# A two-layer encoder with seven-product matmuls: the products in another order, low halves last, two more chunks a layer by seven products, and fourteen more low parts a layer by DMA

## The chip, the cores and the metric

The kernel runs on one core of a Trainium2 chip. The metric is the device time of one execution in microseconds (us). The kernel before was run three times: 1086.85, 1087.01 and 1087.84 us, median 1087.01 us.

## The reference

The reference is an encoder of two residual layers on one sequence of 512 tokens with 1024 features, all in fp32. Layer 0 mixes tokens with a bidirectional gated linear attention, layer 1 with grouped-query softmax attention. Behind each mixer stands a feed-forward part, which is the place of the change:

```python
def conv_ffn(h, w_up, w_conv, b_conv, w_down):
    u = h @ w_up                      # 1024 -> 2 x 2816
    u = lax.conv_general_dilated(u, w_conv[:, None, :], ..., feature_group_count=u.shape[-1]) + b_conv
    val, gate = jnp.split(u, 2, axis=-1)
    return (jax.nn.silu(gate) * val) @ w_down
...
    x = x + conv_ffn(rmsnorm(x, norm_ffn[i]), ffn_w_up[i], ffn_w_conv[i], ffn_b_conv[i], ffn_w_down[i])
```

The convolution is three taps wide, along the tokens, each feature by itself.

## The kernel before

**Three matmuls for one.** TensorE (PE) multiplies in fp32r. To keep fp32 accuracy every weight piece and every activation is kept as a high part (`hi`, a rounded copy) and a low part (`lo`, what the copy left out), and each product is high by high, high by low and low by high: three matmuls. A weight piece is 128x1024 numbers (512 KB). It is loaded from DRAM into a `raw` tile by a DMA on SP's queue; ScalarE (ACT) copies it into a `wh` tile (`split`, L319), and VectorE (DVE) subtracts the copy from the original into a `wl` tile (L320). The other way is `low_dma` (L271, L272): ACT writes the high part, then ACT writes the negative of the rounded number into `wl`, and a DMA on GpSimd's (POOL's) queue adds the original onto it (`flush`, L308). That takes DVE out of it, and costs ACT a second pass and a DMA. Which pieces go this way is set by tables: `UP_DMA` for chunks by three products, `LOW_0`, `LOW_1`, `LOW_2` for the first, second and third piece of a chunk by seven products.

**The feed-forward part.** The 2816 hidden features are 22 chunks of 128; chunk `m` has a value half and a gate half. A chunk not listed in `SEVEN` is a plain one (`plain_up`): two halves of eight blocks by three matmuls of 512 columns, 48 matmuls. A chunk in `SEVEN` (`seven_up`) computes the same by seven products in place of eight (Strassen's way, in Winograd's form, on 2x2 blocks): each product is four blocks by three matmuls of 256 columns, so 84 matmuls. It needs sums of weight blocks, which `summed` makes on DVE (L293, L294, L283): the first piece holds raw weights (products 1 and 4), the second and third hold sums (products 6 and 2, and 7 and 5), the fourth is half as wide (product 3; ACT L285, DVE L286). It also needs its partial results copied in PSUM: `twice` (L1129) copies product 1 into both halves of a bank `r`, so that products 2 and 6 add onto the two halves `r1` and `r2`; `r2` is copied to `r3` after product 6 (L1095) and after product 5 (L1102); `add_seven` (DVE L1132) adds `r3` to the copied product 7. Then come the convolution (ACT L1117, DVE L1118 and L1119), the silu (ACT L1121), the product of the halves (DVE L1122), and, for chunks 0 to 15, `prepare` (L1145 to L1157, L1138, L1139), which makes the operands of the down-projection.

Parts of the down-projection run inside the chunks: `down_part` (four strips by seven products each, onto x in DRAM through POOL's adding DMAs) begins at chunks 9 and 17 (`DOWN_AFTER`). The rest, `PLAIN`, comes at the end.

**What sets the order.** PE, ACT, DVE, POOL and SP each work through their own list of instructions in order; an instruction whose operand isn't ready holds everything behind it on its engine. The program is written chunk by chunk, with weight pieces made some pieces ahead (`PAW`, `PA`); a scheduler of the framework then sets the order on each engine and the buffers. There are five `raw` tiles, six pairs of `wh` and `wl` from chunk 1 to 19 and four after that, and in PSUM three banks `acc`, two `s` and two `pt`.

In the text, "third piece of chunk 14" means the `wh` and `wl` tiles made from the tile `sum` of that chunk.

Of the kernel before, what the change touches and what calls it, by code (L numbers as in the profile page):

```python
# [66 lines left out]
DOWN_AFTER = {9: 0, 17: 1}  # L67


SEVEN = (6, 7, 8, 10, 11, 12, 13, 15, 16, 18, 19, 20, 21)  # L70
UPA = 3
PA = 4
LOADS = 3
# [1 line left out]
INPUT_AT = {2: (0, 1), 3: (2,), 4: (3,)}  # L75
Q_DMA = ()
UP_DMA = (1, 2, 5)
LOW_0 = (7, 8)
LOW_1 = ()
LOW_2 = ()  # L80
STRIP_0 = ()
STRIP_2 = ()
NR = 5
# [17 lines left out]
def hybrid_encoder_kernel(  # L101
# [39 lines left out]
    def bank(tag, n):  # L141
        return pp.tile([P, S], F32, tag=tag, bufs=PS[tag], name=nm(n))
# [33 lines left out]
    class Weights:  # L176
# [127 lines left out]
        def flush(self):  # L304

            for lo, r in self.pending:
                same = lo.dtype == F32R and r.dtype != F32R
                pool.dma_start(lo.bitcast(F32) if same else lo, r, accum_op=ALU.add)  # L308
            self.pending = []

        def split(self, hi, lo, r, pieces=1, first=False):
# [705 lines left out]
    def ffn(layer, norm, cw, nxt):  # L1017
# [22 lines left out]

        def plain_up(m):

            pss = []
            for t in range(2):
                ps = bank("s" if t else "acc", "up")
                feature_tile(*W.half(up[layer], 2 * m + t, max(UPAW if W.wide else UPA, ahead.get((m, t), 1))), norm.hl if m < SWITCH else fresh, ps)
                pss.append(ps)
                if t == 0 and m not in DOWN_AFTER:
                    begin_up(m + 1)
                if t == 0 and m in DOWN_AFTER:  # L1050
                    down.append(down_part(DOWN_AFTER[m], m))
                    next(down[-1])
# [12 lines left out]
        def product(pieces, src, strip, pairs, i, dst, start):  # L1065
            h, o = PLACE[i]
            if h not in pieces:
                pieces[h] = W.piece(src, strip, h, PAW if W.wide else PA)
            wh, wl = pieces[h]
            for j, p in enumerate(pairs):  # L1070
                sl = slice(o + j * P, o + (j + 1) * P)
                mh, ml = p[i]
                for a, (w, m) in enumerate(((wh, mh), (wh, ml), (wl, mh))):
                    mm(dst, w[:, sl], m, start=start and j == 0 and a == 0, stop=j == len(pairs) - 1 and a == 2,  # L1074
                       skip_group_check=True)
            W.flush()

        def begin_up(m):
            if m in SEVEN:
                begun.append(seven_up(m))  # L1080
                next(begun[-1])

        def seven_up(m):

            pieces = {}
            go = lambda *a: product(pieces, up[layer], m, inputs, *a)
            r = bank("pt", "r1")[:, :H]
            go(1, r, True)
            both = bank("acc", "r")
            r1, r2 = both[:, :H], both[:, H:]  # L1090
            twice(both, r)
            yield
            go(6, r2, False)
            r3 = bank("s", "r3")
            act.activation(r3[:, :H], r2, AF.Copy)  # L1095
# [6 lines left out]
            act.activation(r3[:, H:], r2, AF.Copy)  # L1102
            add_seven(d, r3, r4)
            yield 1, d
            begin_up(m + 1)
            go(2, r1, False)
            go(3, r2, False)
            yield 0, both

# [72 lines left out]
        def down_part(part, m):  # L1182

            pairs = [quads.pop(part * NQ + i) for i in range(NQ)]
            st = {}
            pieces = [{} for _ in range(NQ)]
            go = lambda n, *a: product(pieces[n], w_dn, part * NQ + n, pairs, *a)

            def begin(n):
                r = bank("pt", "r1")[:, :H]
                go(n, 1, r, True)
                st[n] = bank("acc", "r")
                twice(st[n], r)

            begin(0)
            yield
            for n in range(NQ):
                r, c, d = st[n], x_home[n][:, :S], x_home[n][:, S:]  # L1200
                r1, r2 = r[:, :H], r[:, H:]
                go(n, 6, r2, False)
                r3 = bank("s", "r3")
                act.activation(r3[:, :H], r2, AF.Copy)
                r4 = bank("pt", "r4")[:, :H]
                go(n, 7, r4, True)
                g, f = tmp("u", "g"), tmp("u", "f")
                twice(f, r4)
                go(n, 4, r3[:, :H], False)
                go(n, 5, r2, False)  # L1210
                act.activation(r3[:, H:], r2, AF.Copy)  # L1211
                add_seven(f, r3, r4)
                W.pending.append((d, f))
                if n + 1 < NQ:
                    begin(n + 1)
                else:
                    begin_up(m + 1)
                go(n, 2, r1, False)
                go(n, 3, r2, False)
                act.activation(g, r, AF.Copy)  # L1220
                W.pending.append((c, g))

        def end(c, ps):
# [375 lines left out]
```

## Time and profile before

| | |
|---|---|
| three runs, median | 1087.01 us (1086.85 to 1087.84) |
| span of the profiled execution | 1085.5 us; its own time lies among these runs, about 1.5 us above the span |
| PE busy | 1077.5 us |
| DVE busy | 888.5 us |
| ACT busy | 721.1 us |
| POOL busy | 136.7 us |
| DMA | 164.52 MB, 152 GB/s on average |
| feed-forward part of layer 0 | about 223 to 555 us |
| attention of layer 1 | about 555 to 741 us |
| feed-forward part of layer 1 | about 741 us to the end |

The span runs from the first to the last instruction. A busy time counts each instruction from start to end. Instructions of one engine overlap a little: the next one may start before the last has ended, so a stretch of work is costed here by the distance from start to start. A busy PE is not PE at its peak, since the ends of matmuls are modelled.

### The profile page before, as it was taken

How to read it: one execution, taken by the hardware profiler on the slowest of the kernel's cores; microseconds unless marked ns; L12 is line 12 of the kernel's file. 1: busy time of each engine (PE TensorE's matmuls, PEld its weight loads, DVE VectorE, ACT ScalarE, POOL GpSimd, SP SyncE). 2: the span in 40 equal slices, each digit the busy share in tenths (PEclk: the TensorE clock that was granted, in tenths of full speed). 3: DMA queues.
4: the chain of work that ended last, by engine and by line, in shares of the span. 5: the costliest groups of instructions: out<-in, count | busy, mean ns of one | idle time of the engine just before them, and what ended most of it. 6: DMA issues, size and time to landing. Idle time of an engine off the chain costs nothing.

```text
span 1085.5 us, 17391 instructions
## 1 busy us (share of the span) xinstructions
PE 1077.5 (99%) x6672; PEld 966.4 (89%) x6672; DVE 888.5 (82%) x1327; ACT 721.1 (66%) x1134; POOL 136.7 (13%) x153
## 2 busy tenths in 40 slices
PE   9999999999999999999999999999999999999998
PEld 8888988888999999999988888888889999999997
DVE  7998967569898899988755588666989889998882
ACT  8679575478775676666574677656877567666660
POOL 0212112021001100010015333002110010001000
PEclk9999999999999999999999999999999999999999
DMA  8744446499545633274767475549863473227542
GB/s 301 187 126 106 122 141 215 154 207 204 127 125 127 145 120 111 77 177 121 252 149 162 127 204 164 164 158 202 206 148 124 105 166 116 100 80 157 136 175 78
DMA packets 55763, 164.52 MB, mean 152 GB/s; under 512 B 6528, under 2 KB 7040, under 8 KB 55680
## 3 DMA queue, kind: packets, MB, share of 16 engines
q1 hardware_dynamic: 36192, 112.66, 32.2%
q0 software_dynamic: 14592, 42.21, 21.7%
q10 hardware_dynamic: 4896, 8.55, 2.1%
q8 instruction: 52, 0.85, 0.3%
q14 instruction: 31, 0.25, 0.1%
HBM read 114.89 MB, written 14.68 MB: 119 GB/s over the span
## 4 chain that ended last, share of the span: by engine, by line
PE 87%; DVE 6%; ACT 3%; DMA 2%; issue 2%; POOL 0%; SPq 0%; DVEq 0%; ACTq 0%; POOLq 0%
PE r L1074 37%; PE op L535 8%; PE vg L652 7%; PE up L482 4%; PE up L483 4%; PE up L484 4%; PE dn L483 2%; PE dn L484 2%; PE dn L482 2%; PE av L509 1%; PE A L482 1%; DVE wl L320 1%; PE A L484 1%; DMA nl<-xr 1%; PE B L484 1%
## 5 line engine op out<-in xcount | busy, mean ns | idle before, releaser
L320 DVE TENSOR_TENSOR wl<-raw,wh 128x1024 fp32r<-128x1024 f32 x156 | 189.8, 1220 | 31.3 <-ACT wh L319 31.1
L319 ACT ACTIVATE wh<-raw 128x1024 fp32r<-128x1024 f32 x156 | 162.6, 1053 | 73.4 <-PE op L535 20.7
L1074 PE MATMUL r<-gu,wh 128*128 128x256 f32 x896 | 161.2, 282 | 0.0
L1074 PE MATMUL r<-xt,wh 128*128 128x256 f32 x832 | 151.1, 283 | 0.4 <-ACT r L1095 0.3
L1074 PEld LDWEIGHTS r<-gu,wh 128*128 128x128 f32 x896 | 139.3, 190 | 1.0 <-ACT r L1211 0.2
L1074 PEld LDWEIGHTS r<-xt,wh 128*128 128x128 f32 x832 | 129.2, 190 | 1.6 <-ACT r L1095 1.1
L1074 PE MATMUL r<-gu,wl 128*128 128x256 f32 x448 | 126.3, 283 | 0.0
L1074 PE MATMUL r<-xt,wl 128*128 128x256 f32 x416 | 117.2, 283 | 0.0
L1074 PE MATMUL r<-nh,wh 128*128 128x256 f32 x312 | 88.8, 285 | 0.3 <-ACT r L1102 0.3
L1074 PE MATMUL r<-nh,wl 128*128 128x256 f32 x312 | 88.2, 283 | 0.0
L1074 PE MATMUL r<-nl,wh 128*128 128x256 f32 x312 | 87.9, 282 | 0.0
L1074 PEld LDWEIGHTS r<-gu,wl 128*128 128x128 f32 x448 | 85.1, 190 | 0.0
L1074 PEld LDWEIGHTS r<-xt,wl 128*128 128x128 f32 x416 | 79.1, 190 | 0.0
L482 PE MATMUL up<-nh,wh 128*128 128x512 f32 x192 | 75.3, 392 | 0.0
L483 PE MATMUL up<-nl,wh 128*128 128x512 f32 x192 | 75.2, 392 | 0.0
L484 PE MATMUL up<-nh,wl 128*128 128x512 f32 x192 | 75.2, 392 | 0.0
L535 PE MATMUL op<-oT,wh 128*128 128x512 f32 x256 | 72.4, 393 | 0.0
L271 ACT ACTIVATE wh<-raw 128x1024 fp32r<-128x1024 f32 x36 | 38.0, 1056 | 38.2 <-PE up L483 11.5
L1074 PEld LDWEIGHTS r<-nh,wh 128*128 128x128 f32 x312 | 59.3, 190 | 2.9 <-ACT r L1102 2.6
L1074 PEld LDWEIGHTS r<-nl,wh 128*128 128x128 f32 x312 | 59.4, 190 | 0.2
L1074 PEld LDWEIGHTS r<-nh,wl 128*128 128x128 f32 x312 | 59.4, 190 | 0.0
L535 PEld LDWEIGHTS op<-oT,wh 128*128 128x128 f32 x256 | 47.4, 188 | 9.7 <-ACT oT L937 0.3
(299 smaller groups left out, 2761.6 us busy)
## 6 DMA issues: line engine op xcount, KB each, us to landing
raw<-in_w_up_dram SPq DMA_DIRECT2D x84, 512.0 KB, 4.6
raw<-in_w_down_dram SPq DMA_DIRECT2D x44, 512.0 KB, 3.7
wl<-raw POOLq DMA_DIRECT2D x20, 512.0 KB, 5.3
wl<-in_w_up_dram POOLq DMA_DIRECT2D x16, 512.0 KB, 7.8
ring<-p ACTq DMA_DIRECT2D x32, 256.0 KB, 2.6
xw<-in_xw_dram SPq DMA_DIRECT2D x8, 512.0 KB, 6.6
raw<-in_w_v_dram SPq DMA_DIRECT2D x8, 512.0 KB, 5.9
raw<-in_w_g_dram SPq DMA_DIRECT2D x8, 512.0 KB, 4.0
```

The lines of the kernel that those rows point to most:

```text
L271: act.activation(hi, r, AF.Copy)
L319: act.activation(hi[:, sl], a, AF.Copy)
L320: dve.tensor_tensor(lo[:, sl], a, hi[:, sl].bitcast(F32), ALU.subtract)
L482: mm(ps, wh, mh, start=start, stop=False)
L483: mm(ps, wh, ml, start=False, stop=False)
L484: return mm(ps, wl, mh, start=False, stop=stop)
L509: mm(ps[j][:, :width], hl[k][i == 2][:, j * P : (j + 1) * P], (wl if i == 1 else wh)[:, sl], start=k == 0 and i == 0, stop=k == KC - 1 and ...
L535: mm(pss[ng][n], wt[:, sl], mv, start=k == late[0][0] and i == 0, stop=k == late[-1][-1] and i == 2)
L652: last = mm(ps[j], m[:, js], w[:, sl], start=i in (1, 7, 2) and p == 0 and a == 0, stop=i in (4, 2, 3) and p == 3 and a == 2, skip_group_c ...
L1074: mm(dst, w[:, sl], m, start=start and j == 0 and a == 0, stop=j == len(pairs) - 1 and a == 2, skip_group_check=True)
```

## The change

1. Chunks 14 and 17 go by seven products too, in both layers.
2. A product multiplies all its high halves first (eight matmuls) and the low halves last (four); before, the low matmul of each of the four blocks followed its two high ones.
3. The order of a chunk's products, 1, 6, 7, 4, 5, then product 1 of the next chunk, 2, 3, becomes 1, 6, 7, 2, 5, product 1 of the next, 4, 3; the strips of the down-projection change in the same way. The copies of partial results are written into the program ahead of the making of further weight pieces.
4. `LOW_0` grows by ten chunks and `LOW_2` by four: fourteen more low parts a layer go by ACT and an adding DMA instead of DVE.
5. `rescale` sends its adding DMAs in a set order on POOL.

```diff
-SEVEN = (6, 7, 8, 10, 11, 12, 13, 15, 16, 18, 19, 20, 21)
+SEVEN = (6, 7, 8) + tuple(range(10, 22))
-LOW_0 = (7, 8)
+LOW_0 = (7, 8, 11, 12, 13, 14, 15, 16, 17, 19, 20, 21)
 LOW_1 = ()
-LOW_2 = ()
+LOW_2 = (13, 14, 16, 17)
...
-            W.todo[at : at + 2] = W.todo[at + 1], W.todo[at]
+            if m not in SEVEN:
+                W.todo[at : at + 2] = W.todo[at + 1], W.todo[at]
...
         def rescale():
+            W.flush()
+            sent = W.sent
...
                 W.low_dma(hi, lo, xr)
+                with tc.issue_after(sent.ins):
+                    W.flush()
...
-        def product(pieces, src, strip, pairs, i, dst, start):
+        def product(pieces, src, strip, pairs, i, dst, start, then=None):
             h, o = PLACE[i]
             if h not in pieces:
-                pieces[h] = W.piece(src, strip, h, PAW if W.wide else PA)
+                pieces[h] = W.piece(src, strip, h, 0)
             wh, wl = pieces[h]
-            for j, p in enumerate(pairs):
-                sl = slice(o + j * P, o + (j + 1) * P)
-                mh, ml = p[i]
-                for a, (w, m) in enumerate(((wh, mh), (wh, ml), (wl, mh))):
-                    mm(dst, w[:, sl], m, start=start and j == 0 and a == 0, stop=j == len(pairs) - 1 and a == 2,
-                       skip_group_check=True)
+            steps = [(j, wh, a) for j in range(len(pairs)) for a in range(2)]
+            steps += [(j, wl, 0) for j in range(len(pairs))]
+            for n, (j, w, a) in enumerate(steps):
+                mm(dst, w[:, o + j * P : o + (j + 1) * P], pairs[j][i][a], start=start and n == 0,
+                   stop=n == len(steps) - 1, skip_group_check=True)
+            if then is not None:
+                then()
+            W.ahead((PAW if W.wide else PA) - len(W.made))
             W.flush()
...
+        def begin(m):
+            if m in DOWN_AFTER:
+                down.append(down_part(DOWN_AFTER[m], m))
+                next(down[-1])
+            else:
+                begin_up(m + 1)
...
-            go(6, r2, False)
             r3 = bank("s", "r3")
-            act.activation(r3[:, :H], r2, AF.Copy)
+            go(6, r2, False, copy(r3[:, :H], r2))
             r4 = bank("pt", "r4")[:, :H]
-            go(7, r4, True)
             d = tmp("u", "u")
-            twice(d, r4)
+            go(7, r4, True, lambda: twice(d, r4))
+            go(2, r1, False)
+            go(5, r2, False, copy(r3[:, H:], r2))
+            begin(m)
             go(4, r3[:, :H], False)
-            go(5, r2, False)
-            act.activation(r3[:, H:], r2, AF.Copy)
             add_seven(d, r3, r4)
             yield 1, d
-            begin_up(m + 1)
-            go(2, r1, False)
             go(3, r2, False)
             yield 0, both
```

The lists below are of layer 0; layer 1 has the same ones. Line numbers of the changed kernel are up to 8 higher in this part (ACT's copies L1095 and L1102 are L1098 there, L1117 is L1124, L1121 is L1128, L1129 is L1136). The number behind a name tells tiles of one name apart.

On ACT, kernel before: the end of chunk 11 (`y_3984`), the copy behind product 6 of chunk 12 (`r_4025<-r_3950`), and the pieces of chunk 13 (`sum_3929`, `raw_3810`).

```order
L1117 ACTIVATE y_3924<-u_3896,cw 128x512
L1117 ACTIVATE y_3984<-r_3824,cw 128x512
L1095 ACTIVATE r_4025<-r_3950 128x256
L1121 ACTIVATE y_3924<-y_3924 128x512
L1129 ACTIVATE u_4044<-r_4027 128x512
L319 ACTIVATE wh_3964<-sum_3929 128x1024
L319 ACTIVATE wh_3932<-raw_3810 128x1024
L319 ACTIVATE wh_4028<-raw_3936 128x1024
L1102 ACTIVATE r_4025<-r_3950 128x256
```

On ACT, kernel after, the same place: the end of chunk 11 (`y_3986`), the pieces of chunk 13 (`sum_3941`, `raw_3821`), and the copy behind product 6 of chunk 12 (`r_4008<-r_3927`).

```order
L1124 ACTIVATE y_3965<-u_3882,cw 128x512
L1124 ACTIVATE y_3986<-r_3798,cw 128x512
L271 ACTIVATE wh_3981<-sum_3941 128x1024
L272 ACTIVATE wl_3982<-sum_3941 128x1024
L319 ACTIVATE wh_3944<-raw_3821 128x1024
L1128 ACTIVATE y_3965<-y_3965 128x512
L1098 ACTIVATE r_4008<-r_3927 128x256
```

The copy stood directly behind the `y`; now two passes for the third piece, one for the second and the silu stand between them.

On PE, kernel before: product 6 of chunk 13, `r_4093`, with the piece `wh_3932`, `wl_3933`.

```order
L1074 MATMUL r_4093<-xt_2434,wh_3932 128x256
L1074 MATMUL r_4093<-xt_2435,wh_3932 128x256
L1074 MATMUL r_4093<-xt_2434,wl_3933 128x256
L1074 MATMUL r_4093<-xt_2442,wh_3932 128x256
L1074 MATMUL r_4093<-xt_2443,wh_3932 128x256
L1074 MATMUL r_4093<-xt_2442,wl_3933 128x256
```

On PE, kernel after: the end of product 1 of chunk 14 (`r_4202`), the last high and the first two low matmuls of its product 7 (`r_4303`, third piece `wh_4127`, `wl_4128`), and the start of product 4 of chunk 13 (`r_4138`).

```order
L1075 MATMUL r_4202<-nh_2239,wl_4043 128x256
L1075 MATMUL r_4303<-xt_2434,wh_4127 128x256
L1075 MATMUL r_4303<-xt_2435,wh_4127 128x256
L1075 MATMUL r_4303<-xt_2442,wh_4127 128x256
L1075 MATMUL r_4303<-xt_2443,wh_4127 128x256
L1075 MATMUL r_4303<-xt_2523,wh_4127 128x256
L1075 MATMUL r_4303<-xt_2524,wh_4127 128x256
L1075 MATMUL r_4303<-xt_2617,wh_4127 128x256
L1075 MATMUL r_4303<-xt_2618,wh_4127 128x256
L1075 MATMUL r_4303<-xt_2434,wl_4128 128x256
L1075 MATMUL r_4303<-xt_2442,wl_4128 128x256
L1075 MATMUL r_4138<-xt_2434,wh_3896 128x256
```

The low matmuls moved behind the eight high ones. Product 7 of chunk 14 is begun before products 4 and 3 of chunk 13 and before its own product 6, and two of its low matmuls too.

On ACT, kernel before: between the copy behind product 5 of chunk 15 (`r_4370`) and the copy behind product 6 of chunk 16 (`r_4513<-r_4438`).

```order
L1102 ACTIVATE r_4370<-r_4306 128x256
L319 ACTIVATE wh_4422<-raw_4352 128x1024
L1129 ACTIVATE r_4438<-r_4421 128x512
L1121 ACTIVATE y_4337<-y_4337 128x512
L285 ACTIVATE wh_4348<-raw_4138 128x512
L1095 ACTIVATE r_4513<-r_4438 128x256
```

On ACT, kernel after, the same place: the copy behind product 5 of chunk 15 (`r_4414`), the third piece of chunk 17 (`sum_4493`), and the copy behind product 6 of chunk 16 (`r_4560<-r_4479`).

```order
L1098 ACTIVATE r_4414<-r_4349 128x256
L285 ACTIVATE wh_4429<-raw_4226 128x512
L1136 ACTIVATE r_4479<-r_4478 128x512
L1124 ACTIVATE y_4517<-u_4434,cw 128x512
L1124 ACTIVATE y_4538<-r_4349,cw 128x512
L271 ACTIVATE wh_4533<-sum_4493 128x1024
L272 ACTIVATE wl_4534<-sum_4493 128x1024
L319 ACTIVATE wh_4496<-raw_4372 128x1024
L1128 ACTIVATE y_4517<-y_4517 128x512
L1098 ACTIVATE r_4560<-r_4479 128x256
```

Where one piece of 128x1024 stood between the two copies, three passes of that size stand now, two of them for one third piece.

More of the change, by code (lines that the diff above doesn't have):

```diff
@@ L307, in flush @@
                 same = lo.dtype == F32R and r.dtype != F32R
-                pool.dma_start(lo.bitcast(F32) if same else lo, r, accum_op=ALU.add)
+                self.sent = pool.dma_start(lo.bitcast(F32) if same else lo, r, accum_op=ALU.add)
             self.pending = []
@@ L1047, in plain_up @@
                 pss.append(ps)
-                if t == 0 and m not in DOWN_AFTER:
-                    begin_up(m + 1)
-                if t == 0 and m in DOWN_AFTER:
-                    down.append(down_part(DOWN_AFTER[m], m))
-                    next(down[-1])
+                if t == 0:
+                    begin(m)
                 if m == 0 and t == 0:
@@ L1189, in down_part, with first @@
             go = lambda n, *a: product(pieces[n], w_dn, part * NQ + n, pairs, *a)
-            def begin(n):
+            copy = lambda o, i: lambda: act.activation(o, i, AF.Copy)
+            def first(n):
                 r = bank("pt", "r1")[:, :H]
-                go(n, 1, r, True)
                 st[n] = bank("acc", "r")
-                twice(st[n], r)
-            begin(0)
+                go(n, 1, r, True, lambda: twice(st[n], r))
+            first(0)
             yield
@@ L1201, in down_part @@
                 r1, r2 = r[:, :H], r[:, H:]
[L1202 removed]
                 r3 = bank("s", "r3")
[L1204 removed]
+                go(n, 6, r2, False, copy(r3[:, :H], r2))
                 r4 = bank("pt", "r4")[:, :H]
[L1206 removed]
                 g, f = tmp("u", "g"), tmp("u", "f")
[L1208 removed]
+                go(n, 7, r4, True, lambda: twice(f, r4))
+                go(n, 2, r1, False)
+                go(n, 5, r2, False, copy(r3[:, H:], r2))
+                if n + 1 < NQ:
+                    first(n + 1)
+                else:
+                    begin_up(m + 1)
                 go(n, 4, r3[:, :H], False)
[L1210 to L1211 removed]
                 add_seven(f, r3, r4)
                 W.pending.append((d, f))
[L1214 to L1220, printed above, removed]
+                go(n, 3, r2, False, lambda: act.activation(g, r, AF.Copy))
                 W.pending.append((c, g))
```

9 lines of the change are left out of this document (4 added, 5 removed).

## Prediction

> **What bounds the kernel now.** I read the busy times first, then stretches of the feed-forward parts, then the chain of waits and PE's own waits.
>
> ```profile
> span 1085.5 us, 17391 instructions
> PE 1077.5 (99%) x6672; PEld 966.4 (89%) x6672; DVE 888.5 (82%) x1327; ACT 721.1 (66%) x1134; POOL 136.7 (13%) x153
> ```
>
> PE is busy for all but 8 us of the span. In the view of stretches the columns are the length, then busy time of PE, weight loads, DVE, ACT and POOL, the clock, the DMA share and GB/s. The first row is the feed-forward part of layer 0, the second a piece of it around chunks 12 to 16, the third that of layer 1 with the tail.
>
> ```profile
> 225.00:555.00 330.00, 330.00 (x2287) 307.96 (x2286) 295.07 (x409) 227.41 (x335) 27.78 (x33) 1.00 0.56 146
> 400.00:450.00 50.00, 50.00 (x333) 45.78 (x332) 49.10 (x73) 33.19 (x53) 0.00 (x0) 1.00 0.30 95
> 741.00:1085.50 344.50, 340.34 (x2330) 315.66 (x2328) 290.47 (x404) 220.47 (x323) 27.03 (x31) 1.00 0.52 136
> ```
>
> In layer 0 PE has no idle time, though around chunks 12 to 16 DVE is busy 49.1 of 50 us. So PE bounds, DVE runs just behind it, and nothing but PE's own work can be saved there: fewer matmul columns shorten the time, and any wait on PE lengthens it one for one. The chain of waits (start, length, what) says the same and gives the price of a matmul, from long runs without a break:
>
> ```profile
> 328.18 75.90 PE r L1074 x636
> 708.71 27.20 PE op L535 x120
> ```
>
> That is 75.90/636 = 0.1193 us for 256 columns and 27.20/120 = 0.2267 us for 512. PE's only waits on another engine in the two parts, from its timeline in layer 1:
>
> ```profile
> 822.49 0.38 PE L1074 MATMUL r<-nh,wh 128*128 128x256 f32 x1 [0.26 <-ACT r L1102]
> 828.95 0.39 PE L1074 MATMUL r<-xt,wh 128*128 128x256 f32 x1 [0.34 <-ACT r L1095]
> ```
>
> **The change part by part.**
>
> *Two more chunks by seven products, twice.* A plain chunk is 48 x 0.2267 = 10.88 us, one by seven products 84 x 0.1193 = 10.02. Four chunks save 4 x 0.86 = **3.4 us**, all on PE's path.
>
> *What moves between DVE and ACT.* Prices are start-to-start distances on ACT's and DVE's timelines:
>
> ```profile
> 421.01 0.37 ACT L1095 ACTIVATE r<-r 128x256 f32<-128x256 f32 x1 [0.53 <-PE r L1074]
> 421.29 0.62 ACT L1138 ACTIVATE gu<-y 128x512 fp32r<-128x512 f32 x1
> 421.81 1.05 ACT L319 ACTIVATE wh<-raw 128x1024 fp32r<-128x1024 f32 x1
> 422.76 0.62 ACT L1138 ACTIVATE gu<-q 128x512 fp32r<-128x512 f32 x1
> 423.28 1.05 ACT L319 ACTIVATE wh<-raw 128x1024 fp32r<-128x1024 f32 x1
> ...
> 425.96 0.38 ACT L1102 ACTIVATE r<-r 128x256 f32<-128x256 f32 x1
> 426.26 1.05 ACT L319 ACTIVATE wh<-raw 128x1024 fp32r<-128x1024 f32 x1
> ```
>
> ```profile
> 421.39 0.42 DVE L1154 TENSOR_TENSOR q<-y,y 128x256 f32<-128x256 f32 x1
> 421.73 0.75 DVE L1118 SCALAR_TENSOR_TENSOR y<-up,cw,y 128x511 f32<-128x511 f32 x1
> 422.39 0.68 DVE L1139 TENSOR_TENSOR gu<-y,gu 128x512 fp32r<-128x512 f32 x1
> 422.99 0.42 DVE L1157 TENSOR_TENSOR y<-y,q 128x256 f32<-128x256 f32 x1
> ...
> 424.02 1.22 DVE L320 TENSOR_TENSOR wl<-raw,wh 128x1024 fp32r<-128x1024 f32 x1
> 425.16 0.42 DVE L1139 TENSOR_TENSOR gu<-y,gu 128x256 fp32r<-128x256 f32 x1
> ```
>
> ACT: 0.30 us for 256 columns, 0.52 for 512, 0.95 for 1024. DVE: 0.34 for 256, 0.60 for 512, 0.66 for 511 with a weight, 1.14 for 1024. By the lists, DVE has 24 fewer low parts (27.4 us) and, for four more chunks by seven products, four times 1.14 + 4 x 0.60 = 3.5 more: 13 us less. ACT gets 28 second passes (26.6 us) and four times 0.95 + 0.52 + 2 x 0.30 + 2 x 0.52 = 3.1: 39 us more, 487 us in 674. Neither is full on the average, so by sums all this would be hidden under PE. But ACT and DVE work in order, and in the lists three places, the same in both layers, have more queued between two PE steps than PE has matmuls to cover. A hand-over costs the tail of an instruction: 0.10 us on ACT (1.05 - 0.95), 0.08 on DVE, 0.16 on PE (the 0.283 of this row less 0.12; the second row, POOL's issues, is used below).
>
> ```profile
> L1074 PE MATMUL r<-xt,wh 128*128 128x256 f32 x832 | 151.1, 283 | 0.4 <-ACT r L1095 0.3
> L308 POOL DMA_DIRECT2D wl<-in_w_up_dram x16 | 14.0, 876 | 151.9 <-ACT wl L272 132.0 <-ACT r L1102 15.7 <-DVE xr L1168 4.2
> ```
>
> *Place A, chunk 12.* Its product 2 waits for the copy behind product 6, which in the new list of ACT stands behind chunk 13's third piece. From the last high matmul of chunk 11's product 3: PE 0.16; DVE low part of chunk 12's fourth piece 0.60 and chunk 13's sum 1.14, 0.08; ACT three passes 2.85, silu 0.52, copy 0.30, 0.10. Together 5.75 us. PE has 35 matmuls for that, 4.18. Wait: **1.6 us**. Without the second pass it would be 0.6.
>
> *Place B, chunk 14.* The low matmuls of product 7 wait for the adding DMA of the third piece. What such DMAs take, from issue to landing: the page's rows, then the DMA line of the tile view for `wl` at 270 to 310 us, for `xt` there, and for `wl` at 730 to 790 us (least, median, most).
>
> ```profile
> wl<-raw POOLq DMA_DIRECT2D x20, 512.0 KB, 5.3
> wl<-in_w_up_dram POOLq DMA_DIRECT2D x16, 512.0 KB, 7.8
> xt<-xr POOLq DMA_DIRECT2D x8, 512.0 KB, 5.3
> ```
>
> ```profile
> DMA to landing us min/median/max: 5.5/5.6/5.8
> ```
>
> ```profile
> DMA to landing us min/median/max: 4.7/4.7/4.7
> ```
>
> ```profile
> DMA to landing us min/median/max: 7.7/7.9/9.0
> ```
>
> The third piece lies in SBUF as `wl<-raw` and `xt<-xr` do, so 4.7 to 5.3; I take 5.0, and 7.9 for a full DMA system. From the last high matmul of chunk 12's product 3: PE 0.16; DVE 0.60 + 1.14 + 0.08; ACT's two passes 1.90 + 0.10; DMA 5.0: 8.98 us. PE has 48 matmuls, 5.73. Wait: **3.25 us** (2.95 to 6.15). That the low half is taken last gives eight matmuls, 0.95 us, and they are counted in the 48.
>
> The Trainium skill, page "DMA: Bandwidth & Descriptors", section "Anatomy of one DMA — SWDGE (gpsimd) path", fits 2.0 us plus bytes over 436e3 for a DMA that POOL issues, an estimate of 3.2 us for 512 KB. By it the wait at B would be 1.45 us and the total 3.6 us less. The trace does not agree for adding DMAs: the fastest median above is 4.7 us.
>
> *Place C, chunks 14 to 16.* From the last matmul of chunk 14's product 4: PE 0.16; DVE from `add_seven` through the operands of the down-projection to chunk 16's sum, five of 512, three of 256 and one of 1024, 5.16, 0.08; ACT five passes of 1024 for chunks 16 and 17 (two of them second ones) and a silu, 5.27, 0.10; DVE three of 512 and chunk 17's sum, 2.94, 0.08; ACT two passes for chunk 17's third piece, one for its second, silu, and the copy behind chunk 16's product 6, 3.67, 0.10. Together 17.4 us. PE has 124 matmuls to product 2 of chunk 16, 14.8. Wait: **2.6 us**; without the three second passes there would be none.
>
> *Edits at nothing.* The ten first pieces: the same sums leave 5.7 us (chunk 8) to 9 us for their DMA behind ACT's second pass, against 5.6 (chunks 15 and 17 only 4, but B's wait falls in between and adds 3); covered by the other products while DMA stays at that, and worth up to 2 us each if it takes 7.9. POOL has 28 more issues of 0.88 us, where it is nearly idle; in its queue they stand behind the strips' adding DMAs, none of which is waited for by PE. The copies in the strips stand 12 matmuls (1.43 us) ahead of their use; short by at most 0.2 us a strip, 0 taken. `rescale`: POOL's list reads the same up to the first strip, so nothing. Layer 1's 0.6 us of PE waits: 0, they may go or stay.
>
> **Sum:** 2 x (1.6 + 3.25 + 2.6) = 14.9, less 3.4, is 11.5 us on the median of 1087.0: **1098.5 us**. The profiled execution's span would go from 1085.5 to 1097.0; the 1.5 us around it stay.
>
> **The rivals.**
>
> *All is covered (faster).* ACT and DVE come to chunk 13 with a lead, since DVE has 6.6 us less to do a layer, and A, B and C shrink. For it: before, copies also stood behind pieces of 0.95 us, DVE was 98% busy, and PE waited for none in layer 0. Against: the three sums start from a PE matmul, so a lead does not help. Price: -3.4, with layer 1's 0.6 recovered -4.0: 1083.0. It decides from 1.7 us of waits a layer downward. Chance 0.18; between, within 2.2 us of no change, 0.07.
>
> *B alone.* If only the late DMA is left and ACT and DVE keep up: 2 x 3.25 - 3.4 = +3.1: 1090.1. Chance 0.20.
>
> *The DMA engines fill up.* The page's queue rows (packets, MB, share of 16 engines) price a load and an adding DMA:
>
> ```profile
> q1 hardware_dynamic: 36192, 112.66, 32.2%
> q0 software_dynamic: 14592, 42.21, 21.7%
> ```
>
> A 512 KB load (0.524 MB) takes 349.5 us/215 = 1.63 us of all 16, an adding one 235.6/80.5 = 2.9. Chunks 13, 14, 16 and 17 need four loads and two adding DMAs, 12.3 us in PE's 10.0. Then B's DMA takes the 7.9 us of the crowded stretch: 2 x 2.9 more, 1104.3. Against it: the waits themselves give the DMA time. Chance 0.10. The Trainium skill, page "Trainium Kernel Development and Optimization", section "Key Constraints", says that DMAs from SP, ACT and POOL share the same 16 engines and interleave; the trace agrees, with 5.6 us for `wl` in one stretch and 7.9 in another.
>
> That the change doesn't do what it says is ruled out by the lists, which have 28 more adding DMAs and 64 fewer matmuls of 512 columns of each of three kinds.
>
> **How the numbers follow.** A measurement of this kernel can tell about 0.2%, 2.2 us. The forecast, all three places, has 0.45; with B alone (0.20) and the full DMA (0.10) slower has 0.75, same 0.07, faster 0.18. The range leaves out the faster case and little else: from 1085.0 (just under no change) to 1105.0 (the full DMA).
>
> **What would show it.** In the profile after, in both layers: PE waits of 1 to 2 us for ACT's 256-column copy in chunk 12, about 3 us for a DMA at `wl` in product 7 of chunk 14, 2 to 3 us for the copy in chunk 16; PE idle up by about 15 us, and its busy time down by 3 to 4. The DMA from `sum` to `wl` lands in about 5 us. I am wrong if PE shows no waits in chunks 12 to 17, or if they are there and the time is not above 1089.

## The result, and the profile after

The changed kernel takes 1120.22 us (median of 5 runs, 1116.33 to 1121.57), the kernel before in the same series 1086.85 us: a ratio of 1.0298, 95% interval 1.0284 to 1.0312. It is slower by about 33 us, three times the 11.5 that were foretold. The profiled execution has a span of 1118.7 us against 1085.5.

The busy times of the kernel after:

```profile
span 1118.7 us, 17940 instructions
PE 1090.2 (97%) x6816; PEld 980.8 (88%) x6816; DVE 879.2 (79%) x1323; ACT 756.8 (68%) x1186; POOL 161.0 (14%) x181
```

PE's idle time went from 8.0 to 28.5 us. Its busy time rose as well, by 12.7 us, although the new matmuls are cheaper by 3.4. So waits are not all: matmuls got slower.

PE's timeline in chunks 12 to 17 of layer 0 shows both (start, length, what, and in brackets the wait ahead of it and its releaser):

```profile
394.03 0.64 PE L1075 MATMUL r<-nh,wl 128*128 128x256 f32 x4
396.26 0.39 PE L1075 MATMUL r<-nh,wh 128*128 128x256 f32 x1 [1.59 <-ACT r L1098]
...
409.49 1.10 PE L1075 MATMUL r<-xt,wh 128*128 128x256 f32 x8
413.98 0.68 PE L1075 MATMUL r<-xt,wl 128*128 128x256 f32 x2 [3.38 <-DMA wl<-sum]
414.46 1.91 PE L1075 MATMUL r<-xt,wh 128*128 128x256 f32 x8
416.17 1.05 PE L1075 MATMUL r<-xt,wl 128*128 128x256 f32 x4
...
435.03 1.10 PE L1075 MATMUL r<-xt,wh 128*128 128x256 f32 x8
438.62 2.08 PE L1075 MATMUL r<-xt,wh 128*128 128x256 f32 x8 [2.49 <-ACT r L1098]
440.50 1.05 PE L1075 MATMUL r<-xt,wl 128*128 128x256 f32 x4
...
447.19 0.64 PE L1075 MATMUL r<-nh,wl 128*128 128x256 f32 x4
449.02 0.39 PE L1075 MATMUL r<-nh,wh 128*128 128x256 f32 x1 [1.19 <-ACT r L1098]
```

The first wait is A, the second B. The third is at product 4 of chunk 15, and the fourth is at product 2 of chunk 16, where C was foretold. Behind B eight matmuls take from 414.46 to 416.17, 0.214 us each where the kernel before needs 0.119, and the same pace stands behind the third wait. The stretches show it as a lower clock (seventh number; the first two rows cover more than 10 us):

```profile
380.00:460.00 80.00, 71.33 (x547) 69.69 (x547) 67.51 (x99) 60.03 (x91) 7.79 (x9) 0.94 0.62 151
400.00:450.00 50.00, 42.92 (x315) 41.86 (x315) 38.67 (x57) 36.46 (x56) 6.05 (x7) 0.90 0.64 153
410.00:420.00 10.00, 6.62 (x43) 6.42 (x42) 4.66 (x7) 5.04 (x8) 1.15 (x2) 0.83 0.71 157
430.00:440.00 10.00, 7.51 (x58) 7.31 (x57) 8.91 (x14) 8.67 (x14) 1.73 (x2) 0.90 0.50 116
440.00:450.00 10.00, 8.81 (x56) 8.61 (x55) 7.29 (x10) 6.33 (x9) 0.86 (x1) 0.76 0.77 185
```

Before, PE had 50.0 us of work at clock 1.00 in the second of these stretches. Layer 1 repeats it, with waits of 1.59, 3.06, 2.49 and 1.94 us.

**Where the 33 us are.** Every distance from one matmul's start to the next is compared with the prices of the long runs (0.119 and 0.227 us). What is above them grew by 36.6 us from the kernel before to the one after; less the 3.4 saved, that is the 33.2 of the span. Of the 36.6, 19.9 are waits that PE's rows name. Of the other 16.7, 10.0 lie in the 8 us behind the five waits with a lower clock after them. The remaining 6.7 are holds of 0.1 to 0.4 us each, which PE's rows don't name as waits. At the products of the strips such holds come to 4.3 us, against 0.4 in the kernel before; the strips' copies on ACT (L1197) release them, or they stand directly behind one that these release. What the other holds wait for isn't shown.

### The profile page after: what moved, and what is told of

It is laid out like the page before. It is cut to its first block, busy times and chain, and to the rows that moved or that the text cites. A ratio compares the mean times of both kernels' runs of the same rounds, so it can differ in the third digit from the quotient of the medians.

```text
span 1118.7 us, 17940 instructions
## 1 busy us (share of the span) xinstructions
PE 1090.2 (97%) x6816; PEld 980.8 (88%) x6816; DVE 879.2 (79%) x1323; ACT 756.8 (68%) x1186; POOL 161.0 (14%) x181
## 3 DMA queue, kind: packets, MB, share of 16 engines
q0 software_dynamic: 18624, 56.89, 28.5%
## 4 chain that ended last, share of the span: by engine, by line
PE 76%; DVE 8%; issue 8%; ACT 4%; DMA 3%; POOL 0%; SPq 0%; DVEq 0%; ACTq 0%; POOLq 0%
PE r L1075 32%; PE op L536 8%; PE vg L653 7%; PE up L483 3%; PE up L484 3%; PE up L485 3%; PE dn L484 2%; PE dn L483 2%; PE dn L485 2%; DVE sum L293 1%; PE av L510 1%; DMA wl<-in_w_up_dram 1%; DVE wl L320 1%; PE A L483 1%; PE A L485 1%
## 5 line engine op out<-in xcount | busy, mean ns | idle before, releaser
L320 DVE TENSOR_TENSOR wl<-raw,wh 128x1024 fp32r<-128x1024 f32 x136 | 165.2, 1217 | 27.1 <-ACT wh L319 26.8
L1075 PE MATMUL r<-gu,wh 128*128 128x256 f32 x896 | 127.3, 284 | 0.2
L1075 PEld LDWEIGHTS r<-gu,wh 128*128 128x128 f32 x896 | 115.1, 190 | 3.4 <-ACT r L1197 1.9
L271 ACT ACTIVATE wh<-raw 128x1024 fp32r<-128x1024 f32 x56 | 59.0, 1054 | 39.2 <-PE up L484 11.5
L1075 PE MATMUL r<-xt,wl 128*128 128x256 f32 x480 | 78.9, 288 | 6.4 <-DMA wl<-sum 6.4
L1075 PEld LDWEIGHTS r<-xt,wl 128*128 128x128 f32 x480 | 67.5, 195 | 6.8 <-DMA wl<-sum 6.8
L308 POOL DMA_DIRECT2D wl<-in_w_up_dram x36 | 31.4, 873 | 284.3 <-ACT wl L272 124.5
L1075 PE MATMUL r<-gu,wl 128*128 128x256 f32 x448 | 71.2, 283 | 0.0
L1124 ACT ACTIVATE y<-u,cw 128x512 f32<-128x512 f32 x42 | 33.8, 810 | 38.3 <-DVE u L1139 37.2
L1075 PE MATMUL r<-nh,wl 128*128 128x256 f32 x360 | 59.2, 286 | 0.3 <-DMA wl<-in_w_up_dram 0.3
L272 ACT ACTIVATE wl<-raw 128x1024 fp32r<-128x1024 f32 x56 | 58.6, 1046 | 0.2 <-PE op L536 0.2
L293 DVE TENSOR_TENSOR sum<-raw,raw 128x1024 f32<-128x1024 f32 x46 | 56.0, 1218 | 0.0
```

Source lines behind the costliest of these rows:

```text
L271: act.activation(hi, r, AF.Copy)
L272: act.activation(lo, r, AF.Copy, scale=-1.0)
L293: dve.tensor_tensor(both(e), both(a21).to_broadcast([P, 2, S]), both(t1), ALU.subtract)
L320: dve.tensor_tensor(lo[:, sl], a, hi[:, sl].bitcast(F32), ALU.subtract)
L1075: mm(dst, w[:, o + j * P : o + (j + 1) * P], pairs[j][i][a], start=start and n == 0, stop=n == len(steps) - 1, skip_group_check=True)
L1124: act.activation(y, u, AF.Identity, scale=w(1), bias=w(3))
```

## The experiments

The theories: (1) the third pieces by DMA make the waits, and each wait costs TensorE clock on top; (2) the new order of the products makes them; (3) two more chunks by seven products are too much for DVE and ACT.

**e1: third pieces back on DVE.**

```diff
-LOW_2 = (13, 14, 16, 17)
+LOW_2 = ()
```

> The changed kernel with the third pieces' low parts back on DVE (LOW_2 empty); the rest of the change stays. Theory 1 (the third pieces' second passes on ACT and their adding DMAs make the waits, and each wait costs about as much again in TensorE clock): at chunk 14 no wait for a DMA from sum, at chunk 12 about 0.6 us instead of 1.6, at chunk 16 none; no clock below 0.95 in chunks 12 to 17; time 1086 us (1083 to 1090), 34 less than the changed kernel. Theory 2 (the new order of the products makes the waits): the waits for ACT's copies stay at 4 us a layer or more, time 1105 or more. Theory 3 (two more chunks by seven products are more than DVE and ACT can serve): DVE, which gets four pieces a layer back, becomes the one that is waited for, time 1100 or more.

Measured: 1097.24 us, ratio to before 1.0096 (1.0081 to 1.0111). PE's waits in the feed-forward parts, in the view of waits (total, times, longest), after and then e1:

```profile
PE r L1075 <- ACT r L1098: 12.2, 9, 2.5
PE r L1075 <- DMA wl<-sum: 6.4, 2, 3.4
PE r L1075 <- DMA wl<-in_w_up_dram: 0.3, 1, 0.3
```

```profile
PE r L1075 <- DMA wl<-in_w_up_dram: 3.1, 5, 1.5
PE r L1075 <- ACT r L1098: 2.3, 5, 0.7
```

So the third pieces cost 23.0 us. The two views differ by 13.5 us of waits, close to the 13.7 that the prediction's sums gave them (2 x (1.0 + 3.25 + 2.6)); the other 9.5 are not in the waits themselves. But 10 us more than before remain, which theory 1 does not explain.

**e2: all fourteen low parts back on DVE.** `LOW_0 = (7, 8)` as well.

> The changed kernel with all fourteen low parts a layer back on DVE (LOW_0 and LOW_2 as before); the new order and the two more chunks stay. Theory 1: about as without the third pieces, 1086 us (1083 to 1092); if the ten first pieces by DMA were needed for DVE's sake, DVE waits of 1 to 3 us a layer in chunks 11 to 17 come in and it is 1088 to 1092. Theory 2: 1105 or more. Theory 3: 1105 or more, with PE waiting for DVE's low parts.

Measured: 1102.25 us, 1.0142 (1.0125 to 1.0158). The ten first pieces by DMA take 5.0 us off. They are no cost; but 15 us are left without any new DMA.

**e3: the three tables in the old order.**

> The kernel before with the three tables of the change alone (SEVEN, LOW_0, LOW_2): two more chunks by seven products and fourteen more low parts a layer by DMA, but the products in the old order with the low halves between the high ones. Theory 1: the wait for the DMA from sum in chunk 14 stays, at 3 to 5 us, and a wait at chunk 16 too; 1105 to 1125 us. Theory 2: no waits over 1 us, 1084 to 1087. Theory 3: 1105 or more.

Measured: 1200.82 us, and nothing to be read: the old code doesn't begin the strips at a chunk by seven products, so 672 matmuls are left out and the weight pieces come in another order. e5 to e7 replace it.

**e4: the new order alone.** The changed kernel with the three tables of before.

> The changed kernel with the three tables of before (SEVEN, LOW_0, LOW_2): the new order of the products, low halves last, alone. Theory 1: no PE wait over 0.6 us in the two feed-forward parts, 1087 us (1085 to 1090). Theory 2: waits for ACT's copies of 4 us a layer or more, 1100 or more. Theory 3: 1087.

Measured: 1090.59 us, 1.0033 (1.0020 to 1.0046). Theory 2 falls as the main cause: the order costs 3.4 us, with no wait over 0.4 us in PE's rows of the feed-forward parts. Most of it lies in holds of 0.06 to 0.21 us at the products of the strips: they come to 3.1 us, against 0.4 before, and the strips' copies on ACT (L1197) release them, or they stand directly behind one that these release.

**e5, e6, e7: the old order with two more chunks, then with the ten first pieces, then with the four third ones.** The old `product` and its order; `seven_up` begins the strips at chunk 17.

```diff
-SEVEN = (6, 7, 8, 10, 11, 12, 13, 15, 16, 18, 19, 20, 21)
+SEVEN = (6, 7, 8) + tuple(range(10, 22))
...
             yield 1, d
-            begin_up(m + 1)
+            begin(m)
```

> The kernel before, products in their old order and low halves between the high ones, with chunks 14 and 17 by seven products; no low part more by DMA. Of the run of the three tables in the old order nothing could be read, since it left out the strips that begin at chunk 17 (672 matmuls); here chunk 17 begins them itself. The new order alone cost 3.4 us, new order and two chunks together 15.0. Theory 1 (the second passes and DMAs are the cost, the two chunks are free): 1083 to 1085 us. Theory 2 (the new order is what makes the two chunks costly): 1083 to 1088. Theory 3 (two chunks more are more than DVE and ACT can serve, in any order): 1095 to 1105, with PE waits in chunks 13 to 18.

> The same, with the ten first pieces by DMA as well (LOW_0 of the change). In the new order these took 5.0 us off. Theory 2: 1082 to 1088. Theory 3: some 5 us less than the same kernel without them, 1090 to 1100. Theory 1: 1083 to 1087.

> The same, with the four third pieces by DMA too: the whole change but for the order of the products and of the low halves. Theory 1: the third pieces cost 20 to 30 us more than the same kernel without them, in any order, since the waits behind ACT's second passes and for the DMA stay. Theory 2: under 8 us more. Theory 3: 20 to 30 more as well.

Medians of all, in us (before is 1086.7 to 1087.3 in each series):

| | old order | new order |
|---|---|---|
| tables of before | 1087 (before) | 1090.6 (e4) |
| two chunks more | 1100.3 (e5), 1.0113 (1.0098 to 1.0129) | 1102.3 (e2) |
| and ten first pieces by DMA | 1097.1 (e6), 1.0088 (1.0073 to 1.0104) | 1097.2 (e1) |
| and four third pieces by DMA | 1118.4 (e7), 1.0283 (1.0268 to 1.0299) | 1120.2 (the change) |

The two chunks cost 13 us in the old order and 11.7 in the new, where 3.4 were to be gained; the third pieces cost 21 to 23 in either order. The changed order is worth 0 to 3.4 us and no cause of the rest. In e5 PE waits for pieces that DVE's sums hold up. PE's timeline, then ACT's at the same place, where the copies into `wh` themselves wait for DVE, which has no idle time there:

```profile
429.22 0.28 PE L1072 MATMUL r<-nh,wl 128*128 128x256 f32 x1
430.98 0.50 PE L1072 MATMUL r<-xt,wh 128*128 128x256 f32 x2 [1.47 <-ACT wh L319]
432.24 0.80 PE L1072 MATMUL r<-xt,wh 128*128 128x256 f32 x2 [0.76 <-ACT wh L319]
```

```profile
429.87 1.06 ACT L319 ACTIVATE wh<-sum 128x1024 fp32r<-128x1024 f32 x1 [0.44 <-DVE sum L293]
431.13 2.00 ACT L319 ACTIVATE wh<-raw 128x1024 fp32r<-128x1024 f32 x2 [0.20 <-DVE raw L294]
```

**e8: idle time filled with matmuls.** The high half of product 7 is done three times in chunks 14 and 16.

```diff
-LOW_2 = (13, 14, 16, 17)
+LOW_2 = (13, 14, 16, 17); TIMES = {14: 3, 16: 3}
...
-            steps = [(j, wh, a) for j in range(len(pairs)) for a in range(2)]
+            steps = (TIMES.get(strip, 1) if i == 7 else 1) * [(j, wh, a) for j in range(len(pairs)) for a in range(2)]
...
-                mm(dst, w[:, o + j * P : o + (j + 1) * P], pairs[j][i][a], start=start and n == 0,
+                mm(dst, w[:, o + j * P : o + (j + 1) * P], pairs[j][i][a], start=start and n % 8 == 0 and w is wh,
```

> The changed kernel, with the eight high matmuls of product 7 done three times over in chunks 14 and 16 of both layers, each time begun anew, so the result is the same: 16 matmuls, 1.9 us, stand ahead of the wait for the DMA from sum (3.4 us) and of the wait at product 4 of chunk 15 (2.5 us), in time in which PE is idle anyway. Theory 1 (a wait of over 2 us lowers TensorE's granted clock behind it, which costs about 2 to 4 us a time more): the waits shrink by 1.9 us each, the clock stays at 1.00 behind them, and the time falls by 6 to 10 us to 1110 to 1114, with 64 more matmuls. Its rival (the slow pace behind the waits comes from what DVE, ACT and the DMA do there, not from the wait): the pace stays at 0.21 us a matmul and the time within 2 us of the changed kernel.

Measured: 1112.48 us, 1.0231 (1.0214 to 1.0248): 7.7 us less than the changed kernel, with 64 matmuls more. PE's timeline at the places of B and of the third wait, and the stretches:

```profile
410.39 4.20 PE L1075 MATMUL r<-xt,wh 128*128 128x256 f32 x32
414.43 0.64 PE L1075 MATMUL r<-xt,wl 128*128 128x256 f32 x4
...
433.20 3.00 PE L1075 MATMUL r<-xt,wh 128*128 128x256 f32 x24
436.55 1.22 PE L1075 MATMUL r<-xt,wh 128*128 128x256 f32 x8 [0.34 <-ACT r L1098]
```

```profile
410.00:420.00 10.00, 9.98 (x82) 9.60 (x81) 7.87 (x12) 7.83 (x13) 1.73 (x2) 1.00 0.77 165
430.00:440.00 10.00, 9.66 (x81) 9.45 (x80) 8.20 (x13) 7.61 (x12) 1.73 (x2) 1.00 0.53 109
440.00:450.00 10.00, 8.32 (x66) 7.75 (x65) 9.84 (x16) 8.47 (x14) 0.86 (x1) 1.00 0.77 196
```

The clock stays at 1.00 where it was 0.83, 0.90 and 0.76, with DVE, ACT and the DMAs about as busy as in the changed kernel or busier. In layer 1 one of the places keeps its slow stretch, behind a wait of 1.74 us. Over the whole span named waits fell by 9.8 us and the fill takes 64 x 0.119 = 7.6, a net 2.2; the other 6.1 of the 8.3 us of span lie in no named wait and fit the pace got back. So a wait can lower the clock behind it, and PE pays that on top.

**e9, e10: DVE relieved by way of ACT and DMA.** `Q_DMA = (5, 6, 7)` on e5 and on e2.

> The kernel with the two more chunks in the old order and no low part more by DMA (1100.3 us), with the low parts of the operands of the down-projection made in chunks 11, 13 and 15 by ACT and DMA instead of DVE (Q_DMA = 5, 6, 7). That takes three subtractions of 512 columns and one of 256 each off DVE, 3 x 2.2 = 6.6 us a layer between chunks 11 and 16, and what is made there is needed by PE only in the strips of chunk 17, so that no DMA stands in PE's way. Theory 3, as the last runs leave it (with two more chunks DVE has more work between chunks 11 and 17 than PE has, and PE waits for the difference): the time falls by 6 to 13 us to 1087 to 1094. Its rival (the two chunks cost by ACT's queue ahead of PE, and not by DVE's load): ACT gets 5.6 us a layer more, and the time stays at 1098 or rises.

> The same step on the kernel with the new order and the two chunks (1102.3 us without it). Theory 3: 1088 to 1096. Rival: 1100 or more.

Measured: 1109.34 us, 1.0196 (1.0175 to 1.0217), and 1116.54 us, 1.0266 (1.0248 to 1.0285): 9 and 14 us worse than without. The waits in e9:

```profile
PE r L1072 <- ACT r L1100: 11.6, 6, 2.8
PE r L1072 <- DMA gu<-y: 5.1, 2, 2.9
```

The passes that left DVE stand on ACT ahead of copies that PE waits for, and the DMA of the last operands came too late for the strips of chunk 17. So this didn't tell whether DVE's load was the cause: it brought costs of its own, and the forecast for a relieved DVE (1087 to 1096) was missed.

**e11: longer waits in the kernel before.**

```diff
-LOW_2 = ()
+LOW_2 = (); COPIES = {7: 11, 13: 15, 19: 19, 21: 25}
...
-            act.activation(r3[:, :H], r2, AF.Copy)
+            for _ in range(COPIES.get(m, 1)): act.activation(r3[:, :H], r2, AF.Copy)
```

> The kernel before, with ACT's copy behind product 6 repeated 11, 15, 19 and 25 times in chunks 7, 13, 19 and 21 of both layers (0.30 us each), so that PE waits at product 4 for about 2, 3, 4 and 6 us with nothing else changed. Theory 1 on the clock: behind the waits of over 2 us some microseconds of matmuls go at 0.21 us instead of 0.12, 2 to 4 us more for each wait, and the time is 35 to 55 us above the kernel before. Its rival (no clock loss from a wait): the pace behind them is 0.12 us and the time is only the waits above the kernel before, about 30 us.

Measured once: 1129.02 us, 42 above before. The instructions were ordered anew, so the waits came at other places and shorter than planned. Named waits grew by 24.3 us, and all that lies above the prices of the long runs by 41.4: here too 17 us are not in the waits. It agrees with theory 1 on the clock; its lengths can't be read as planned.

**e12: sums left out.** e5 without DVE's sums for the second and third pieces of chunks 12 to 17.

```diff
-                e = pair("raw", NR, F32, "sum")
+                bare = 11 < i < 18
+                e = t1 if bare else pair("raw", NR, F32, "sum")
...
-                with tc.issue_after(self.last.ins) if self.last else ExitStack():
-                    dve.tensor_tensor(both(e), both(a21).to_broadcast([P, 2, S]), both(t1), ALU.subtract)
-                dve.tensor_tensor(a21, a11, e[:, S:], ALU.subtract)
+                with tc.issue_after(self.last.ins) if self.last and not bare else ExitStack():
+                    bare or dve.tensor_tensor(both(e), both(a21).to_broadcast([P, 2, S]), both(t1), ALU.subtract)
+                bare or dve.tensor_tensor(a21, a11, e[:, S:], ALU.subtract)
```

> The kernel with the two more chunks in the old order (1100.3 us), leaving out the sums of weight blocks for the second and third pieces of chunks 12 to 17, so that those pieces are made from the raw tiles (part of the computation is left out; the output is another). That takes 6 x 1.74 = 10.4 us a layer off DVE and puts nothing on ACT or on a DMA. If DVE's work between chunks 11 and 17 is what PE waits for: 1083 to 1088 us. If ACT's queue or the length of the chain from PE through DVE and ACT back to PE is: 1094 or more.

Measured: 1083.34 us, 0.9971 (0.9958 to 0.9984), 3.4 us less than before: just what the matmuls of the four chunks save. The stretch of chunks 12 to 17 in the kernel before, in e5 and in e12:

```profile
380.00:460.00 80.00, 80.00 (x582) 75.66 (x582) 78.06 (x111) 54.68 (x84) 0.00 (x0) 1.00 0.32 100
```

```profile
380.00:460.00 80.00, 75.02 (x605) 73.86 (x604) 78.25 (x110) 56.32 (x88) 0.00 (x0) 0.98 0.30 92
```

```profile
380.00:460.00 80.00, 80.00 (x668) 79.66 (x668) 78.23 (x112) 61.32 (x98) 0.00 (x0) 1.00 0.31 96
```

DVE is busy 78 of 80 us in all three, so its busy share doesn't tell them apart. Before and in e12 PE is full beside it; in e5 PE does 75.0. So theory 3 holds in this form: the cost of the two chunks goes when DVE's sums of this stage go. Whether they cost by DVE's load or by their place in the chain ahead of the copies isn't separated: e12 takes both away, and with them one tile a chunk and a rule on the order of the sums (`issue_after`). Load alone isn't the whole. In e6 seven first pieces of chunks 11 to 17 leave DVE, 7 x 1.14 = 8.0 us a layer, and only 3.2 us come back; PE then waits five times, 4.0 us in all, for the DMAs of the first pieces (`wl<-in_w_up_dram`).

**e13, e14, e15: one chunk alone, 17, 14 or 9**, in the old order.

> The old order with chunk 17 alone by seven products more. If DVE's work in the stage decides: the strips right behind chunk 17 leave DVE time, so this chunk costs less than chunk 14, 1087 to 1092 us. If a chunk by seven products costs the same anywhere: 1093.

> The old order with chunk 14 alone by seven products more, in the middle of the stage in which DVE is 98 per cent busy. If DVE's work in the stage decides: 3.5 us more work and 0.9 less time for it a layer, less 1 to 2 us of slack, 1090 to 1096 us. If a chunk costs the same anywhere: 1093.

> The old order with chunk 9 alone by seven products more. It stands ahead of the first strips, in which DVE was 73 per cent busy in the kernel before, from 340 to 360 us. If DVE's work in the stage decides: no loss, 1085 to 1088 us, the best case for another chunk by seven products. If a chunk costs the same anywhere: 1093.

Measured: 1097.20 us, 1.0093 (1.0076 to 1.0110); 1099.66 us, 1.0118 (1.0101 to 1.0134); 1091.27 us, 1.0040 (1.0025 to 1.0055), chunks 17 and 14 above both values expected of them, chunk 9 between its two. All three have a wait that e5 lacks, at the start of layer 1. PE in e15, behind it the pace of 0.43 us for 512 columns:

```profile
768.98 0.39 PE L484 MATMUL up<-nl,wh 128*128 128x512 f32 x1
773.03 0.80 PE L485 MATMUL up<-xhl,wl 128*128 128x512 f32 x1 [3.67 <-DMA wl<-in_w_up_dram]
773.62 0.63 PE L483 MATMUL up<-xhl,wh 128*128 128x512 f32 x1
774.05 0.63 PE L484 MATMUL up<-xhl,wh 128*128 128x512 f32 x1
```

**e16, e17, e18: the same, and the rotation of the tiles moved on by one in layer 1.** Every third pair of weight tiles comes from the wide buffers, by a counter. One chunk more shifts it, and in POOL's list the second piece's DMA then stands behind the four of `rescale`.

```diff
-                W.loads, W.wide = LOADS_FFN, 1
+                W.loads, W.wide = LOADS_FFN, 1; W.turn += layer
```

> Chunk 9 alone by seven products more, with the counter by which every third pair of weight tiles comes from the wide buffers set on by one at chunk 1 of layer 1. In the run without that, the second weight piece at the start of layer 1 got its tile late, its adding DMA stood in POOL's queue behind the four of rescale, and PE waited 3.7 us for it and went at a lower clock for 2.8 more; now that DMA stands ahead of them again, as in the kernel before. If this wait is a side effect of the tiles' rotation and chunk 9 itself costs nothing: 2 x 0.86 us faster than the kernel before, 1085 to 1086 us. If the wait belongs to the added work: 1090 to 1092.

> Chunk 17 alone, with the same setting of the counter; in the run without it the same wait stood at the start of layer 1. Side effect: 1097.2 less some 5.5, 1091 to 1092.5 us, so that chunk 17 itself costs 4 to 6 us where 1.7 were to be gained. Otherwise: 1096 to 1098.

> Chunk 14 alone, with the same setting of the counter. Side effect: 1099.7 less some 6.5, 1092 to 1094 us, so that chunk 14 itself costs 5 to 7 us. Otherwise: 1098 to 1101.

Measured: e16 (chunk 9) 1085.08 us, 0.9980 (0.9971 to 0.9989); e17 (chunk 17) 1094.84 us, 1.0072 (1.0058 to 1.0085); e18 (chunk 14) 1095.03 us, 1.0082 (1.0065 to 1.0099). The wait was a side effect of the rotation, worth 2.4 to 6.2 us. Chunk 9, by sums of the same kind but ahead of the full stage (DVE busy 14.6 of 20 us at 340 to 360 us before), gains 1.95 us, about what the columns say (1.7), and is the version to keep. Chunk 17 costs as much as chunk 14: that the strips behind it would give DVE time was wrong. They came out 2.3 and 1.0 us above the ranges expected. Each alone costs 8 us, both together 13; why the second costs less isn't shown.

## Why the prediction was wrong, point by point

**Where the sum went wrong.** The prediction has 14.9 us of waits less 3.4, 11.5. The changed kernel's rows have 17.7 us in the waits A, B and C, 2.2 in other named waits, 10.0 of lower clock behind the waits and 6.7 of short holds, less 3.4: 33.2. So of the 21.7 us that are missing, 10.0 fall to a term that the prediction had no room for, 6.7 to holds that it put at nothing, 2.8 to A, B and C, and 2.2 to waits elsewhere. The runs without some of the edits come to the same total by another road: in the old order the two chunks cost 13.0, the first pieces give back 3.2, the third pieces cost 21.3, and the new order 1.9.

*"Any wait on PE lengthens it one for one":* the step that failed and cost most. The lower clock behind five waits costs some 10 us in the changed kernel, and e8 took 6.1 us off beyond the waits. PE's busy time, foretold to fall by 3 to 4, rose by 12.7, by that and by the short holds.

*Two more chunks, -3.4 us: the columns right, the cover wrong.* e12 and e16 gain about what the matmuls say. But "by sums all this would be hidden under PE", with the loads taken on the average of 674 us, failed too where the two chunks come without the DMAs. The prediction quoted DVE at 49.1 of 50 us around chunks 12 to 16, and drew from it only that PE bounds. In that stage a plain chunk is what lets DVE keep up. By the prediction's own prices a chunk by seven products gives DVE 1.14 + 4 x 0.60 = 3.5 us more and PE 0.9 less time to cover it. Two chunks are 8.8 us in a stage with 80 - 78.1 = 1.9 us of slack: 6.9 us a layer, 14 in all. e5 lost 16.4 (its 13 and the 3.4 not gained). The balance is an estimate and on the low side: for one chunk it gives 4.9, and 9.5 were lost in e17. In the changed kernel the fourteen low parts by DMA take this load off DVE, which is busy 67.5 of 80 us there; what PE then waits for are A, B and C.

*A, 1.6 us:* measured 1.59 in both layers. *B, 3.25 us:* 3.38 and 3.06, with the DMA at 4.5 us instead of 5.0:

```profile
wl<-sum POOLq DMA_DIRECT2D x4, 512.0 KB, 4.5
```

The page's estimate of 3.2 us (the Trainium skill, "DMA: Bandwidth & Descriptors", "Anatomy of one DMA — SWDGE (gpsimd) path") lies below the medians of all adding DMAs of 512 KB shown here and in the prediction, as it did before.

*C, 2.6 us at product 2 of chunk 16:* there 1.19 in layer 0 and 1.94 in layer 1, and in both layers 2.49 before it at product 4 of chunk 15. The chain's ACT part was right, but it ran past a copy, that behind product 5 of chunk 15, for which PE waits as well:

```profile
432.94 1.06 ACT L271 ACTIVATE wh<-sum 128x1024 fp32r<-128x1024 f32 x1 [0.94 <-DVE sum L293]
433.91 1.04 ACT L319 ACTIVATE wh<-raw 128x1024 fp32r<-128x1024 f32 x1
434.85 1.04 ACT L272 ACTIVATE wl<-sum 128x1024 fp32r<-128x1024 f32 x1
435.80 1.04 ACT L271 ACTIVATE wh<-raw 128x1024 fp32r<-128x1024 f32 x1
436.74 1.04 ACT L272 ACTIVATE wl<-raw 128x1024 fp32r<-128x1024 f32 x1
437.69 0.61 ACT L1128 ACTIVATE y<-y 128x512 f32<-128x512 f32 x1
438.21 0.36 ACT L1098 ACTIVATE r<-r 128x256 f32<-128x256 f32 x1
```

Five passes and a silu stand ahead of the copy that ended at 438.57; PE went on at 438.62. Two waits in a chain were counted as one. Together A, B and C were 17.7 us instead of 14.9. (The terms listed for C add up to 17.56 us and not 17.4, so that its wait would have been 2.8; that changes nothing else.)

*Edits at nothing.* The first pieces: no cost, and even a gain where the two chunks load DVE (3 to 5 us). The copies in the strips and the order: 3.4 us in e4, where 0 was taken; the prediction's own "at most 0.2 us a strip" is 3.2 us over the sixteen strips of both layers. `rescale`: nothing was seen, and it was not tried apart.

*The rivals.* None held. With all covered the time would have fallen; B alone is ruled out by the other waits; the DMA engines did not fill, since B's DMA took 4.5 us and not 7.9.

## What to carry to other kernels

Set an engine's load against the bound in the stage where the work lands, not on average: where a second engine is busy 98% of the time, the slow work of the first is what lets it keep up, and a saving on the first belongs where the second has time to spare (chunk 9 here). Price a TensorE wait of some 2.5 us or more at itself plus the 1.4 to 3 us that half pace cost behind most of them here. A counter that hands out buffers is part of an edit: look whether the edit shifts it somewhere else.

## What the runs showed of the hardware

A wait can lower TensorE's granted clock for the matmuls behind it. From the feed-forward part of layer 0 on, in the changed kernel and the experiments, all 25 waits of 2.9 us or more were followed, within 8 us, by some 2 to 6 us at about half pace (0.21 us for 256 columns), and so were 12 of 16 between 2.4 and 2.9 us (18 of these 41 are in e3, whose time can't be read but whose rows can). Of those between 1.0 and 2.4 us some were, often with another short wait beside them. The same wait can do it or not. In e9 both layers have one of 2.81 us at the same place, first layer 0 with its stretch, then layer 1:

```profile
405.73 0.51 PE L1072 MATMUL r<-xt,wh 128*128 128x256 f32 x2 [2.81 <-ACT r L1100]
...
936.01 0.51 PE L1072 MATMUL r<-xt,wh 128*128 128x256 f32 x2 [2.81 <-ACT r L1100]
```

```profile
400.00:410.00 10.00, 7.19 (x58) 6.79 (x57) 9.65 (x13) 8.58 (x15) 2.62 (x3) 1.00 0.87 195
930.00:940.00 10.00, 7.19 (x48) 6.99 (x48) 9.13 (x12) 8.53 (x15) 2.62 (x3) 0.84 0.83 188
```

The clock is 1.00 in the one and 0.84 in the other. The Trainium skill, page "TensorE: Matmul & The Clock Gate", section "Part 1: The HAM clock gate", tells of a gate that halves the clock by the activity in a window of about 3.4 us that runs free of the program. The trace agrees with the half pace and the chance in it; of the 20 slow stretches outside e3 six lasted 3.3 to 3.5 us, the others between 2.5 and 5.8. It does not agree with the page's limit of about 3.4 us for a harmless gap: here 2.4 to 2.9 us were enough in 12 of 16 places.
